# Contrast adjustment on one core: third tile loaded in two pieces, first store held for the larger piece, whole-tile sums on ScalarE for the last three tiles

## The chip, the cores and the metric

The kernel runs on one core of one Trainium2 chip. The metric is the device time of one execution in microseconds (us), as the median of several runs. One execution was also recorded by the hardware profiler; its span runs from the first instruction to the last, and its device time is a little longer than that span.

## The reference

```python
def reference(x, factor):                       # x: (16, 3, 512, 512) float32, factor = 1.5
    mean = np.mean(x, axis=(2, 3), keepdims=True)
    return np.clip(mean + factor * (x - mean), 0, 1).astype(np.float32)
```

There are 48 images (16 batches of 3 channels) of 262,144 pixels each. Every image is stretched around its own mean and cut to 0..1. So every pixel is read once and written once, 50.33 MB each way, and nothing of an image can be written before its mean is known.

## The kernel before

**Tiles.** An image is cut into 16 rows of 16,384 pixels (64 KB each). A tile is 128 such rows, one for each partition, so eight images; there are six tiles of 8.39 MB, numbered 0 to 5. They live in a ring of three buffers (`ring`), so tile 3 takes the buffer of tile 0, and so on: only half of the data is on the chip at a time.

**One tile's work.** `load` (L77) issues the DMA into the ring. `add` sums each row: VectorE reduces the first `SUM` = 4352 columns (L85), and ScalarE copies the other 12,032 columns onto themselves with an accumulated sum (L89). TensorE multiplies the row sums by `blockw`, a 128x128 matrix with (1 - factor)/262144 in blocks of 16x16 (L100), which adds up the 16 rows of each image and gives every partition its image's shift, (1 - factor) * mean, in `bias`. VectorE then makes two passes over the tile in place: times factor plus shift (L103), and the clip to 0..1 (L106). `store` (L80) issues the DMA to `out`.

**Tile 0** is handled in smaller parts so that work starts early. It is loaded in pieces of 8, 24 and 32 KB of each row, summed in two halves, and passed over and stored in two pieces: the first `SHORT` = 2048 columns (8 KB of each row, 1 MB in all), then the other 56 KB of each row.

**Order.** The order is written out by hand (`manual_schedule`): five DMAs load tiles 0 to 2, then the three tiles are computed and stored, then tiles 3 to 5 are loaded, computed and stored. All DMAs, loads and stores alike, are issued by SyncE (SP) on one queue, and SP issues them in program order. A DMA that must wait for an engine or for another transfer (a store for VectorE's clip, a load for the store that frees its buffer) therefore holds up every DMA that stands behind it in SP's order. Each DMA goes over 16 DMA engines, each with eight of the 128 rows, one packet a row.

Of the kernel before, what the change touches and what calls it, by code (L numbers as in the profile page):

```python
# [1 line left out]

# [4 lines left out]


P = 128  # L10
ROW = 16384
HALF = ROW // 2
BUFS = 3
SHORT = 2048
SUM = 4352


@with_exitstack
def kernel(
    ctx: ExitStack,  # L20
    tc: tile.TileContext,
    x: bass.AP,
    factor: float,
    out: bass.AP,
):

    nc = tc.nc
    f32 = mybir.dt.float32  # L30
    Alu = mybir.AluOpType
    Act = mybir.ActivationFunctionType

    B, C, H, W = x.shape
    n_img, n_pix = B * C, H * W
    ppi = n_pix // ROW
    per_tile = P // ppi
    n_tiles = n_img // per_tile
    assert ppi * ROW == n_pix and per_tile * n_tiles == n_img

    factor = float(factor)
    wconst = (1.0 - factor) / float(n_pix)

    x_f = x.rearrange("b c h w -> (b c h w)")
    out_f = out.rearrange("b c h w -> (b c h w)")

    def dram(ap, t, c0=0, c1=ROW):
        return bass.AP(tensor=ap.tensor, offset=t * P * ROW + c0, ap=[[ROW, P], [1, c1 - c0]])

    consts = ctx.enter_context(tc.tile_pool(name="consts", bufs=1))  # L50
    xpool = ctx.enter_context(tc.tile_pool(name="xpool", bufs=1))
    small = ctx.enter_context(tc.tile_pool(name="small", bufs=1))
    psum = ctx.enter_context(tc.tile_pool(name="psum", bufs=1, space=bass.MemoryType.PSUM))


    sums = small.tile([P, 4 * n_tiles], f32, name="sums")
    bias = psum.tile([P, n_tiles], f32, name="bias")

    blockw = consts.tile([P, P], f32, name="blockw")
    blocks = blockw.rearrange("p (a b) -> p a b", b=ppi)  # L60
    nc.gpsimd.memset(blockw, wconst)  # L61
    for base, step in ((0, -ppi), (ppi - 1, ppi)):
        nc.gpsimd.affine_select(  # L63
            out=blocks,
            in_=blocks,
            compare_op=Alu.is_ge,
            fill=0.0,
            base=base,
            pattern=[[step, per_tile], [0, ppi]],
            channel_multiplier=1 if step < 0 else -1,  # L70
        )


    ring = xpool.tile([P, BUFS, ROW], f32, name="ring")

    def load(t, c0=0, c1=ROW):
        nc.sync.dma_start(out=ring[:, t % BUFS, c0:c1], in_=dram(x_f, t, c0, c1))  # L77

    def store(t, c0=0, c1=ROW):
        nc.sync.dma_start(out=dram(out_f, t, c0, c1), in_=ring[:, t % BUFS, c0:c1])  # L80

    def add(t, col, c0, c1, c2):
        xt = ring[:, t % BUFS, :]
        own = sums[:, 4 * t + col : 4 * t + col + 2]
        nc.vector.tensor_reduce(  # L85
            out=own[:, 0:1], in_=xt[:, c0:c1], axis=mybir.AxisListType.X, op=Alu.add
        )
        part = xt[:, c1:c2]
        nc.scalar.activation(out=part, in_=part, func=Act.Copy, accum_out=own[:, 1:2])  # L89
        return [own[:, 1:2], own[:, 0:1]]  # L90

    def compute(t, *cuts):
        xt = ring[:, t % BUFS, :]
        if t == 0:
            parts = add(t, 0, 0, SUM, HALF) + add(t, 2, HALF, HALF + SUM, ROW)
        else:
            parts = add(t, 0, 0, SUM, ROW)
        shift = bias[:, t : t + 1]
        for k, part in enumerate(parts):
            nc.tensor.matmul(shift, blockw, part, start=k == 0, stop=k == len(parts) - 1)  # L100
        for c0, c1 in zip((0, *cuts), (*cuts, ROW)):
            part = xt[:, c0:c1]
            nc.vector.tensor_scalar(  # L103
                out=part, in0=part, scalar1=factor, scalar2=shift, op0=Alu.mult, op1=Alu.add
            )
            nc.vector.tensor_scalar(  # L106
                out=part, in0=part, scalar1=0.0, scalar2=1.0, op0=Alu.max, op1=Alu.min
            )
            store(t, c0, c1)

    with tc.manual_schedule():
        load(0, 0, SHORT)
        load(0, SHORT, HALF)
        load(0, HALF, ROW)
        load(1)
        load(2)
        compute(0, SHORT)
        compute(1)
        compute(2)
        load(3)  # L120
        load(4)
        load(5)
        compute(3)
        compute(4)
        compute(5)


# [1 line left out]
_INS = ['x', 'factor']  # L129
_OUTS = [((16, 3, 512, 512), 'float32')]  # L130

_NUMBERS = {'factor': 1.5}


# [26 lines left out]
```

## Time and profile before

| | |
|---|---|
| median of 3 runs | 239.52 us (239.28 to 239.88) |
| profiled execution | 239.05 us, span 237.3 us |
| bytes | 50.33 MB read, 50.33 MB written |
| VectorE busy | 137.4 us |
| ScalarE busy | 59.9 us |
| TensorE busy | 7.9 us |
| first store issued by SP | at 30.52 us |
| loads of tiles 3, 4, 5 issued | at 94.24, 101.08, 120.82 us |
| stores of tiles 3, 4, 5 issued | at 168.97, 191.81, 214.64 us |

"Busy" counts the time in which an engine executes instructions, and says nothing of whether that time matters. Times of instructions are counted from the start of the span. A DMA has two times of interest: when SP issues it, and when it lands, that is, when its completion is signalled to whoever waits for it. In between it lies in the queue behind earlier DMAs for most of the time: the median load of a whole tile lands 57.7 us after its issue. The view of DMA over time gives, for each slice, the mean busy share of the 16 DMA engines in tenths and what they moved in GB/s; in short slices a packet's bytes are counted where the packet starts.

### The profile page before, as it was taken

What the parts mean: (1) busy time and instruction counts of PE and PEld (TensorE: products, weight loads), DVE (VectorE), ACT (ScalarE), POOL (GpSimd) and SP (SyncE); (2) the same over time, 40 slices, a digit from 0 to 9 for tenths busy, and PEclk for the clock granted to TensorE, in tenths of its full rate; (3) what the DMA queues carried; (4) which work ended last, traced back from release to release, by engine and by line L of the source; (5) the groups of instructions that cost most, each with busy time, mean ns of one, the idle gap of its engine ahead of it and who ended that gap; (6) DMA issues with size and microseconds to landing.
All of it is one profiled execution on the core that took longest, in us unless ns stands there. A gap on an engine that the chain in (4) does not pass through costs nothing.

```text
span 237.3 us, 186 instructions
## 1 busy us (share of the span) xinstructions
PE 7.9 (3%) x28; PEld 6.9 (3%) x28; DVE 137.4 (58%) x21; ACT 59.9 (25%) x15; POOL 1.1 (0%) x7
## 2 busy tenths in 40 slices
PE   0010100010001000000000000100000000000000
PEld 0010100010001000000000000100000000000000
DVE  0071899949998998000000043499989998991000
ACT  2051300980492000000000049319509800000000
POOL 1000000000000000000000000000000000000000
DMA  7999989899799798989899998989899998989894
GB/s 289 418 442 442 530 353 530 353 486 398 331 464 454 341 530 353 530 353 519 365 442 442 398 486 353 530 354 530 353 475 409 431 453 376 508 353 530 353 530 177
DMA packets 2160, 100.66 MB, mean 424 GB/s; under 512 B 240, under 2 KB 240, under 8 KB 240
## 3 DMA queue, kind: packets, MB, share of 16 engines
q1 hardware_dynamic: 2160, 100.66, 98.7%
HBM read 50.33 MB, written 50.33 MB: 424 GB/s over the span
## 4 chain that ended last, share of the span: by engine, by line
DVE 43%; DMA 36%; ACT 9%; PE 2%; SPq 1%; issue 0%; DVEq 0%; ACTq 0%
DMA ring<-in_x_dram 36%; DVE ring L103 18%; DVE ring L106 18%; ACT ring L89 9%; DVE sums L85 6%; PE bias L100 2%; SPq L77 1%; SPq L80 0%; DVEq L103 0%; ACTq L89 0%
## 5 line engine op out<-in xcount | busy, mean ns | idle before, releaser
L89 ACT ACTIVATE ring<-ring 128x12032 f32<-128x12032 f32 (+1 forms) x7 | 58.0, 8280 | 128.2 <-DMA ring<-in_x_dram 128.2
L85 DVE TENSOR_REDUCE sums<-ring 128x1 f32<-128x4352 f32 x7 | 32.8, 4683 | 63.9 <-DMA ring<-in_x_dram 63.9
L103 DVE TENSOR_SCALAR ring<-ring,bias 128x16384 f32<-128x16384 f32 (+2 forms) x7 | 52.8, 7538 | 12.9 <-PE bias L100 12.9
L106 DVE TENSOR_SCALAR ring<-ring 128x16384 f32<-128x16384 f32 (+2 forms) x7 | 52.3, 7476 | 0.2
L100 PE MATMUL bias<-sums,blockw 128*128 128x1 f32 x28 | 7.9, 360 | 189.1 <-ACT ring L89 175.4
L100 PEld LDWEIGHTS bias<-sums,blockw 128*128 128x128 f32 x28 | 6.9, 314 | 190.0 <-ACT ring L89 159.4
L89 ACT ACT_TABLE_LOAD x1 | 1.3, 1283 | 0.8 <-PEq L142 0.8
L89 ACT ACTIVATION_READ_ACCUMULATOR ring<-ring 128x1 f32 x7 | 1.3, 187 | 0.0
L63 POOL TENSOR_SCALAR_AFFINE_SELECT blockw<-blockw 128x128 f32<-128x128 f32 x2 | 0.7, 340 | 0.1
L61 POOL MEMSET blockw<- 128x128 f32 x1 | 0.2, 204 | 0.3 <-POOLq L142 0.3
L142 POOL MEMSET const-bfloat16-1.0<- 128x1 bf16 x1 | 0.1, 102 | 0.0
L142 POOL MEMSET const-uint8-127<- 128x1 uint8 x1 | 0.1, 102 | 0.0
L142 POOL MEMSET const-float32-0.0<- 128x1 f32 x1 | 0.1, 98 | 0.3 <-issue 0.3
L142 POOL MEMSET const-float32-1.0<- 128x1 f32 x1 | 0.1, 98 | 0.0
## 6 DMA issues: line engine op xcount, KB each, us to landing
out_dram<-ring SPq DMA_DIRECT2D x1, 7168.0 KB, 35.9
ring<-in_x_dram SPq DMA_DIRECT2D x1, 4096.0 KB, 20.8
ring<-in_x_dram SPq DMA_DIRECT2D x1, 3072.0 KB, 11.6
ring<-in_x_dram SPq DMA_DIRECT2D x1, 1024.0 KB, 4.7
out_dram<-ring SPq DMA_DIRECT2D x1, 1024.0 KB, 34.3
ring<-in_x_dram SPq DMA_DIRECT2D x5, 57.7
out_dram<-ring SPq DMA_DIRECT2D x5, 27.0
```

The lines of the kernel that those rows point to most:

```text
L61: nc.gpsimd.memset(blockw, wconst)
L63: nc.gpsimd.affine_select(out=blocks, in_=blocks, compare_op=Alu.is_ge, fill=0.0, base=base, pattern=[[step, per_tile], [0, ppi]], channel ...
L77: nc.sync.dma_start(out=ring[:, t % BUFS, c0:c1], in_=dram(x_f, t, c0, c1))
L85: nc.vector.tensor_reduce(out=own[:, 0:1], in_=xt[:, c0:c1], axis=mybir.AxisListType.X, op=Alu.add)
L89: nc.scalar.activation(out=part, in_=part, func=Act.Copy, accum_out=own[:, 1:2])
L100: nc.tensor.matmul(shift, blockw, part, start=k == 0, stop=k == len(parts) - 1)
L103: nc.vector.tensor_scalar(out=part, in0=part, scalar1=factor, scalar2=shift, op0=Alu.mult, op1=Alu.add)
L106: nc.vector.tensor_scalar(out=part, in0=part, scalar1=0.0, scalar2=1.0, op0=Alu.max, op1=Alu.min)
L142: nc = _bacc.Bacc("TRN2", target_bir_lowering=False, num_devices=1)
```

## The change

Three things change.

1. Tile 2 is loaded by two DMAs: the first 58 KB of each row (`ROW - TAIL` = 14,848 columns), then the last 6 KB (`TAIL` = 1536 columns).
2. The first store (the 1 MB piece of tile 0) gets one more thing to wait for: the landing of the 58 KB piece of tile 2. As SP issues in order, the DMAs behind it wait too.
3. For tiles 3 to 5, ScalarE sums all 16,384 columns and VectorE's reduction is left out, so TensorE has one product instead of two. For tiles 0 to 2 the split of the sum stays; only the order in which the two instructions are written, and the columns of `sums` that they use, are exchanged.

```diff
+TAIL = 1536
...
     def add(t, col, c0, c1, c2):
         xt = ring[:, t % BUFS, :]
         own = sums[:, 4 * t + col : 4 * t + col + 2]
+        part = xt[:, c1:c2]
+        nc.scalar.activation(out=part, in_=part, func=Act.Copy, accum_out=own[:, 0:1])
+        if c0 == c1:
+            return [own[:, 0:1]]
         nc.vector.tensor_reduce(
-            out=own[:, 0:1], in_=xt[:, c0:c1], axis=mybir.AxisListType.X, op=Alu.add
+            out=own[:, 1:2], in_=xt[:, c0:c1], axis=mybir.AxisListType.X, op=Alu.add
         )
-        part = xt[:, c1:c2]
-        nc.scalar.activation(out=part, in_=part, func=Act.Copy, accum_out=own[:, 1:2])
-        return [own[:, 1:2], own[:, 0:1]]
+        return [own[:, 0:1], own[:, 1:2]]
 
-    def compute(t, *cuts):
+    def compute(t, *cuts, after=None):
         xt = ring[:, t % BUFS, :]
         if t == 0:
             parts = add(t, 0, 0, SUM, HALF) + add(t, 2, HALF, HALF + SUM, ROW)
         else:
-            parts = add(t, 0, 0, SUM, ROW)
+            parts = add(t, 0, 0, SUM if t < BUFS else 0, ROW)
...
-            store(t, c0, c1)
+            out_dma = store(t, c0, c1)
+            if c0 == 0 and after is not None:
+                tc.add_manual_dep(
+                    out_dma.ins,
+                    after.ins.name,
+                    mybir.DependencyInfo(mybir.DependencyClass.Sync, mybir.DependencyReason.DATA),
+                    reason="the first store follows the loads",
+                )
 
     with tc.manual_schedule():
         load(0, 0, SHORT)
         load(0, SHORT, HALF)
         load(0, HALF, ROW)
         load(1)
-        load(2)
-        compute(0, SHORT)
+        most = load(2, 0, ROW - TAIL)
+        load(2, ROW - TAIL, ROW)
+        compute(0, SHORT, after=most)
```

More of the change, by code (lines that the diff above doesn't have):

```diff
@@ L76, in load @@
     def load(t, c0=0, c1=ROW):
-        nc.sync.dma_start(out=ring[:, t % BUFS, c0:c1], in_=dram(x_f, t, c0, c1))
+        return nc.sync.dma_start(out=ring[:, t % BUFS, c0:c1], in_=dram(x_f, t, c0, c1))
     def store(t, c0=0, c1=ROW):
-        nc.sync.dma_start(out=dram(out_f, t, c0, c1), in_=ring[:, t % BUFS, c0:c1])
+        return nc.sync.dma_start(out=dram(out_f, t, c0, c1), in_=ring[:, t % BUFS, c0:c1])
     def add(t, col, c0, c1, c2):
```

## The prediction

> **What bounds the kernel now.** I read the page first, then the share of each transfer, then the few microseconds around the first change from loading to storing, then the waits around the edits. The page:
>
> ```profile
> span 237.3 us, 186 instructions
> ...
> PE 7.9 (3%) x28; PEld 6.9 (3%) x28; DVE 137.4 (58%) x21; ACT 59.9 (25%) x15; POOL 1.1 (0%) x7
> ...
> q1 hardware_dynamic: 2160, 100.66, 98.7%
> ```
>
> One queue moves 100.66 MB and its packets fill 98.7% of what 16 DMA engines have; VectorE is busy for 58%, ScalarE for 25%. The bound is the queue. The chain of waits credits VectorE with 43%, but that chain follows who issued a DMA; it doesn't show that the queue still had other work. So an edit pays only if it takes time out of the stream of transfers.
>
> That stream runs in order of issue. I cut the span at the landings of its transfers. A landing is an issue plus its time to landing (the page's DMA issues), or the start of the work that waited for it. The windows view (columns: window, its length, busy time of five engines, clock, DMA share, GB/s):
>
> ```profile
> 22.56:41.91 19.35, 1.17 (x4) 1.00 (x4) 18.58 (x5) 3.50 (x2) 0.00 (x0) 1.00 1.00 434
> 41.91:62.38 20.47, 1.01 (x4) 0.93 (x4) 17.36 (x4) 10.32 (x2) 0.00 (x0) 1.00 0.92 375
> ...
> 81.75:101.06 19.31, 0.00 (x0) 0.00 (x0) 11.96 (x2) 0.00 (x0) 0.00 (x0) 1.00 1.00 434
> ...
> 159.12:178.48 19.36, 1.17 (x4) 1.00 (x4) 18.57 (x4) 10.32 (x2) 0.00 (x0) 1.00 1.01 433
> 178.48:197.82 19.34, 1.18 (x4) 1.00 (x4) 18.55 (x4) 10.32 (x2) 0.00 (x0) 1.00 1.00 434
> ```
>
> In order: load of tile 1, load of tile 2, store of tile 1, load of tile 5, store of tile 3. A tile of 8.39 MB takes 19.31 to 19.36 us at 434 GB/s, except tile 2, the last load before the first store: 20.47, which is 1.12 more. (The view books a packet's bytes at its start, so 375 understates that window and the next one overstates.) No other transfer stands out: the two windows left out after the store of tile 1 are 19.74 and 18.96, and sum to two tiles. Outside the stream there is only the start. So 1.12 us is about all that the queue can still give.
>
> Where in tile 2? The DMA view from 50 to 66 us, 40 slices of 0.4 us:
>
> ```profile
> DMA  0390000390000390000590000000279999993003
> GB/s 0 164 2458 0 0 0 0 164 2458 0 0 0 0 164 2458 0 0 0 0 164 2458 0 0 0 0 0 0 0 123 328 430 471 389 410 983 1639 143 0 0 143
> ```
>
> Each pair "164 2458" is the 16 engines starting one 64 KB row. The pairs come six slices apart, 2.4 us. After the last one, at 58.0 to 58.4, the next packets (the 8 KB rows of the first store) only begin at 61.2 and are common from 61.6: the last row of tile 2 held the engines over a microsecond too long. From 61.6 the store runs at some 430 GB/s. That first store was issued at 30.52 and lay behind the loads for 30 us:
>
> ```profile
> 30.52 63.63 SPq L80 DMA_DIRECT2D out_dram<-ring  x4
> ...
> 62.40 10.23 ACT L89 ACTIVATE ring<-ring 128x12032 f32<-128x12032 f32 x1 [10.15 <-DMA ring<-in_x_dram]
> ...
> 168.97 46.01 SPq L80 DMA_DIRECT2D out_dram<-ring  x3
> ```
>
> The other change from loading to storing, at 178.5, also had its store queued early (168.97), with rows of 64 KB, and lost nothing (19.36, then 19.34). So what disturbs seems to be many small store rows that wait right behind the last load row.
>
> **The change part by part.**
>
> *First store held until 58 KB of each row of tile 2 have landed.* At the stream's rate, 58 of 64 KB take 19.35 x 58/64 = 17.54 us, so that part lands at 41.91 + 17.54 = 59.45. SP goes on 0.02 us after a landing (the load of tile 5 was issued at 120.82; the store before it landed at 93.82 + 27.0 = 120.82, at 120.80 by the cut). The first store is then issued at 59.47 instead of 30.52, after nearly all of tile 2 is in. What this removes: up to 1.12 us.
>
> Its price is the risk that the queue runs dry. 6 KB of each row are left as cover: 19.35 x 6/64 = 1.81 us. The only row with an issue into an empty queue is the first load: issued at 0.80, 1 MB, landed 4.7 us later. If the first store needed as long, it would land at 59.47 + 4.7 = 64.17. In an unbroken stream tile 2 is in at 41.91 + 19.35 = 61.26 and the store's 1 MB (8.39 MB in 19.35 gives 2.42) lands at 63.68. The gap would be 0.49. The other end is 0: the engines are running, not cold, and the store reads on-chip memory. Below 0 is excluded, since 434 GB/s is the most that any cut shows. I take the middle, 0.25, because the one row is like in size and row length but is a load at a cold start.
>
> Can the disturbance remain in part? The first load's packets began at 1.8 us (DMA view of the first 8 us), 1.0 after issue, so the store's rows could reach an engine from 60.5 on, and tile 2's data end by about 60.9: tile 1 landed at 41.91, but its last rows had given way to tile 2's by 41.5 (the pair at 50.4 to 51.2, less four rows of 2.42), so a landing comes some 0.4 us after the data, and 61.26 - 0.4 = 60.9. The overlap is at most some 0.4 of a row's 2.42 us, or 0.4/2.42 x 1.12 = 0.19 us. It comes on an engine in place of the gap, not on top, so 0 to 0.49 stays the span of both.
>
> Queued behind the waiting store on SP are the second store (ready at 45.8), the store of tile 1 (ready at 70.9), and the later loads from 94.2. The second store then issues at about 59.9, and the stream needs it at 63.7 less the 1 us of lead; it is covered by 2.8 us. Nobody else moves. VectorE and ScalarE never wait for a store in this half, and the loads that reuse the buffers are issued at 94.24 as before, set by VectorE's end at 93.75.
>
> *Load of tile 2 in two pieces.* One more issue on SP, 0.4 us at 2.8 to 3.3 us, hidden behind 60 us of loads. The second piece has 6 KB rows. The nearest row is the store of tile 0, split in 1 MB and 7 MB: landings at 30.52 + 34.3 = 64.82 and 45.82 + 35.9 = 81.72, from 62.40, so 19.32 in all, as an unsplit store. Cost 0, at most a few hundredths.
>
> The Trainium skill speaks against this piece: "DMA: Bandwidth & Descriptors", section "Rules for kernel authors", asks for at least 1 MiB per DMA, and "Anatomy of one DMA" (the GpSimd path) charges a fixed 2.0 us or so for each (fitted on DMAs issued from GpSimd). The piece has 0.75 MiB; at that price the sum would be about 240.65. The two store pieces above show no such fee inside a full queue, and the trace decides.
>
> *ScalarE adds tiles 3 to 5 whole.* ScalarE takes 10.23 us for 12032 columns and 3.40 for 3840, so (10.23 - 3.40)/8192 = 0.834 ns a column and 13.86 us for 16384. VectorE loses three reductions of 4.68, TensorE three pairs of instructions. Per tile: landing, 13.86, 0.19 for the accumulator, 0.05, one product 0.60, 0.11, then VectorE's 17.49 and 0.07 to the store's issue. Tile 3 (landing 139.76 - 0.87 = 138.89): store issued at 171.3, before 168.97; the stream reaches it when load 5 lands, at 177.6. Tile 4 (158.25): 190.6, before 191.8; due at 197.0. Tile 5 (177.6): 210.0, before 214.64; due at 216.3. Every store stays queued 6 us ahead, so all of it lies under the transfers: cost 0 and gain 0. If that cover were gone, tile 3 would cost 2.3 us (3.2 counted from the earlier landing). The other order of the two adds within a tile changes no engine's own order.
>
> **Sum.** 1.12 - 0.25 = 0.87. The profiled execution had 239.05 us, a span of 237.30 and 1.75 around it; after the change its span would be 236.43 and its time 238.18. The median of the runs is 0.47 above it, so 239.52 - 0.87 = **238.65 us**. With 0.49 of gap it is 238.89, with none 238.40.
>
> **The rivals.**
>
> *The 1.12 us is the first store's own start, not its place behind the loads* (slower). It is the first write to `out`, and the second change of direction, which shows none, is not the first. Then the cost stays, and the wait adds its gap: 239.52 + 0.49 = 240.0. The wait loses from the point where gap and what is left of the cost exceed 1.12. Passing 0.3% (0.72 us here, about what a measurement of this kernel can tell from no change) needs a lead of the store 0.23 us longer than the first load's. Against it: the late bytes are those of the load, and the store's packets run at full rate from the first slice.
>
> *The disturbance moves to the 6 KB rows.* The store's 8 KB rows reach engines that still have small load rows in hand and cost half or more of the 1.12: 239.0 to 239.5. For it: store rows are as small as before, and an engine can be up to 0.4 us behind another. Against it: the overlap is short.
>
> *The change does nothing.* Holding the store doesn't matter, since the late row has another cause, such as VectorE's pass over tile 1 from 53.4 to 71 (columns as many were processed from 76 to 94 with the queue at 434, which speaks against it): 239.5.
>
> **How the numbers follow.** The forecast gets 0.60, the first-store rival 0.20, the moved disturbance 0.15, nothing 0.05. Faster than 238.80 are 0.57 from the forecast and 0.01 from the edge of the moved disturbance, 0.58. Slower than 240.24 is half of the first-store rival, 0.10. The rest, 0.32, is within 0.3%. The forecast's own range is 238.4 to 238.9; to leave out no more than 2 in 10 it has to take in the second and third rival and the near edge of the first: 238.3 to 239.8.
>
> **What the next profile would show.** Right: the first store issued near 59.5, ScalarE on tile 2 near 61.3 instead of 62.40, tile 2's 58 KB rows evenly spaced at 2.2 us with no empty microsecond after the last, store of tile 0's first piece landed by 64.0, all later landings 0.9 earlier, and stores of tiles 3 to 5 issued near 171.3, 190.6 and 210.0 with the DMA share still about 1. It is wrong if the slices between 60.5 and 62 hold more than 0.5 us without packets (lead too long), if tile 2's last piece lands after 61.8 (disturbance still there), or if any store after 170 us is issued after the queue has reached it.

## The result, and the profile after

The changed kernel is slower: a median of 240.19 us (239.52 to 241.94, 14 runs) beside 239.40 (239.07 to 239.88, 14 runs) of the kernel before, a ratio of 1.0041 with a 95% interval of 1.0028 to 1.0054. The forecast was 238.65 us in a range of 238.3 to 239.8. A second set of runs gave 241.02 (6 runs), 1.0065 (1.0052 to 1.0078). The runs also scatter more than those of the kernel before: three of the 14 took 241.30 to 241.94 us, the other eleven 239.52 to 240.42.

The profiled execution took 241.83 us, with a span of 240.1; that is one of the three, so its profile shows the losses at their larger end. A second profile below is milder (240.84 us), but none of the eleven was profiled. The page first, with the lines that answer to those of before:

```profile
span 240.1 us, 167 instructions
...
PE 6.3 (3%) x22; PEld 5.4 (2%) x22; DVE 123.6 (51%) x18; ACT 70.8 (29%) x15; POOL 1.1 (0%) x7
...
q1 hardware_dynamic: 2304, 100.66, 97.9%
```

VectorE is 13.8 us less busy and ScalarE 10.9 more, as the third edit says, and none of it reached the span. The queue moves the same bytes, and its packets fill 97.9% of the span where they filled 98.7%. In windows cut at the landings (the order is load of tile 1, load of tile 2, store of tile 1, store of tile 2, load of tile 3, load of tile 5, store of tile 3):

```profile
22.70:42.05 19.35, 1.17 (x4) 1.00 (x4) 18.58 (x5) 3.50 (x2) 0.00 (x0) 1.00 0.99 428
42.05:61.46 19.41, 1.02 (x4) 0.93 (x4) 16.33 (x3) 10.32 (x2) 0.00 (x0) 1.00 0.94 402
80.88:100.21 19.33, 0.00 (x0) 0.00 (x0) 12.96 (x2) 0.00 (x0) 0.00 (x0) 1.00 1.00 434
100.21:120.42 20.21, 0.00 (x0) 0.00 (x0) 0.00 (x0) 0.00 (x0) 0.00 (x0) 1.00 0.99 412
120.42:140.80 20.38, 0.00 (x0) 0.00 (x0) 0.00 (x0) 0.00 (x0) 0.00 (x0) 1.00 0.96 415
160.12:181.33 21.21, 0.59 (x2) 0.50 (x2) 19.36 (x3) 13.95 (x2) 0.00 (x0) 1.00 1.06 439
181.33:200.68 19.35, 0.59 (x2) 0.50 (x2) 15.64 (x3) 13.95 (x2) 0.00 (x0) 1.00 1.01 437
```

The second line is the success: tile 2 takes 19.41 us where it took 20.47. The others are where it went: the store of tile 2 takes 20.21 (before 19.74), the load of tile 3 20.38 (18.96), the load of tile 5 21.21 (19.36). The two windows of the kernel before for the store of tile 2 and the load of tile 3:

```profile
101.06:120.80 19.74, 0.00 (x0) 0.00 (x0) 0.00 (x0) 0.00 (x0) 0.00 (x0) 1.00 0.98 425
120.80:139.76 18.96, 0.00 (x0) 0.00 (x0) 0.00 (x0) 0.00 (x0) 0.00 (x0) 1.00 1.02 442
```

All three longer windows lie at the two later changes of direction, from storing to loading at about 120 us and from loading to storing at about 178. VectorE and ScalarE did nothing at all from 100 to 140.

The DMA view from 50 to 66 us (40 slices of 0.4) shows the first crossing as it was meant to be:

```profile
DMA  9300399000993003990002899899999999000093
GB/s 1485 148 0 0 148 1485 742 0 0 0 891 1336 148 0 0 148 1782 445 0 0 0 108 353 492 430 369 425 425 471 410 389 410 1720 881 0 0 0 0 2150 143
```

The starts of the 58 KB rows come in bursts 2.2 us apart, then at 58.4 the 6 KB rows begin at about 430 GB/s, and the 8 KB rows of the first store follow at 60.5 with no empty slice. The store was issued at 59.70, and its wait on SP reads in the waits view as:

```profile
SPq L81 <- DMA ring<-in_x_dram: 55.7, 1, 55.7
```

Now the second crossing, the same view from 112 to 128 us, before and then after:

```profile
DMA  9900009900009930009930009930009970009970
GB/s 983 1638 0 0 0 0 983 1638 0 0 0 0 983 1475 164 0 0 0 983 1475 164 0 0 0 983 1475 164 0 0 0 655 1638 328 0 0 0 655 1638 328 0
```

```profile
DMA  0000790000990000009900403900303930303930
GB/s 0 0 0 0 328 2294 0 0 0 0 328 2294 0 0 0 0 0 0 1147 1311 0 0 164 0 164 2294 0 0 164 0 164 2130 164 0 164 0 164 2130 164 0
```

Before, every burst of row starts follows the last by six slices (2.4 us), straight through the crossing. After, the burst at 116.0 is followed by the next at 119.2, eight slices later: the last row of the store of tile 2 held its engine for most of a microsecond too long. One engine fell behind the others as well (the lone 164 three slices, 1.2 us, behind each burst, first at 120.8).

To compare kernels I take a **loss at a crossing**: the time between two landings around it, less what the transfers between take in an undisturbed stretch (19.345 us for the load of a tile, 19.30 for the store of one at the second crossing and 19.31 at the third, 2.43 for 1 MB). A landing here is when a DMA's completion is counted; each of the 16 engines counts by itself, and the table gives the median engine and, after the stroke, the last one, which sets the end. A crossing is a change of direction, and "held" means held as in the change, behind a piece of 58 KB of each row with 6 KB left as cover, unless the table says otherwise. All in us, from one profile each.

| kernel | first crossing (61) | second (120) | third (178) | ratio to before, 95% interval |
|---|---|---|---|---|
| before | 1.07 / 1.16 | 0.03 / 0.06 | 0.06 / 0.04 | |
| the change | 0.15 / 0.12 | 0.87 / 1.97 | 0.90 / 1.84 | 1.0041 (1.0028 to 1.0054) |
| the change, second profile | 0.27 / 0.29 | 0.97 / 1.46 | 0.95 / 1.33 | 1.0065 (1.0052 to 1.0078) |
| split and hold alone | 0.52 / 0.34 | 0.82 / 1.73 | 0.97 / 1.34 | 1.0068 (1.0052 to 1.0084) |
| ScalarE edit alone | 1.49 / 1.56 | 0.02 / -0.02 | 0.17 / 0.10 | 0.9998 (0.9989 to 1.0006) |
| split alone | 1.35 / 1.32 | 0.05 / 0.10 | 0.03 / 0.19 | 0.9993 (0.9984 to 1.0002) |
| hold with 24 KB of cover | 1.56 / 1.56 | 0.03 / 0.05 | 0.22 / 0.46 | 1.0002 (0.9993 to 1.0011) |
| first and third held | 0.27 / 0.31 | 1.02 / 1.59 | 0.58 / 0.10 | 1.0032 (1.0022 to 1.0043) |
| second alone held | 1.40 / 1.43 | 0.70 / 0.99 | 1.13 / 1.52 | 1.0089 (1.0075 to 1.0103) |
| all three held | 0.56 / 0.77 | 1.02 / 1.04 | 0.33 / 0.23 | 1.0009 (0.9998 to 1.0019) |
| stores held in mid-stream, 6 KB of cover | 1.41 / 1.42 | 0.84 / 0.99 | 0.97 / 1.21 | 1.0101 (1.0078 to 1.0123) |
| the same, 24 KB of cover | 1.35 / 1.34 | 0.01 / 0.02 | 0.03 / 0.05 | 0.9997 (0.9988 to 1.0006) |
| small store at 42 us | 1.64 / 1.71 | 0.05 / 0.06 | 0.04 / 0.06 | 1.0001 (0.9992 to 1.0009) |
| small store at 5 us | 0.34 / 0.54 | -0.02 / 0.09 | 0.07 / 0.22 | 1.0021 (1.0008 to 1.0035) |

The profile's span grew by 2.8 us, and the last engine's terms add up to it: -1.04 at the first crossing, +1.91 at the second, +1.80 at the third, and 0.14 of a later start, 2.81 in all.

### The profile page after: what moved, and what is told of

It is laid out like the page before. It is cut to its first block, busy times and chain, and to the rows that moved or that the text cites. A ratio compares the mean times of both kernels' runs of the same rounds, so it can differ in the third digit from the quotient of the medians.

```text
span 240.1 us, 167 instructions
## 1 busy us (share of the span) xinstructions
PE 6.3 (3%) x22; PEld 5.4 (2%) x22; DVE 123.6 (51%) x18; ACT 70.8 (29%) x15; POOL 1.1 (0%) x7
## 3 DMA queue, kind: packets, MB, share of 16 engines
q1 hardware_dynamic: 2304, 100.66, 97.9%
## 4 chain that ended last, share of the span: by engine, by line
issue 29%; ACT 17%; DVE 7%; another core or an unknown queue 5%; PE 0%; ACTq 0%
ACT ring L87 17%; DVE ring L106 4%; DVE ring L109 4%; PE bias L103 0%; ACTq L87 0%; ACTq L167 0%
## 5 line engine op out<-in xcount | busy, mean ns | idle before, releaser
L87 ACT ACTIVATE ring<-ring 128x16384 f32<-128x16384 f32 (+2 forms) x7 | 68.8, 9834 | 123.8 <-issue 69.1
L90 DVE TENSOR_REDUCE sums<-ring 128x1 f32<-128x4352 f32 x4 | 18.7, 4682 | 18.0 <-DMA ring<-in_x_dram 18.0
L103 PE MATMUL bias<-sums,blockw 128*128 128x1 f32 x22 | 6.3, 360 | 189.7 <-ACT ring L87 185.3
L103 PEld LDWEIGHTS bias<-sums,blockw 128*128 128x128 f32 x22 | 5.4, 314 | 190.5 <-ACT ring L87 169.2
```

The source lines that it names most:

```text
L90: nc.vector.tensor_reduce(out=own[:, 1:2], in_=xt[:, c0:c1], axis=mybir.AxisListType.X, op=Alu.add)
```

## The experiments

All of them are edits of the kernel before, except where the change itself is the base.

**Which edit does it?** Three parts of the change, and the change again. The hold without the ScalarE edit:

```diff
-            parts = add(t, 0, 0, SUM if t < BUFS else 0, ROW)
+            parts = add(t, 0, 0, SUM, ROW)
```

> The split load and the held first store, without the ScalarE edit (tiles 3 to 5 are summed by VectorE and ScalarE as before). Theory A (the toll moves): a change of direction of the queue costs about 1 us when the 16 DMA engines cross it in step with the next transfer already queued; the first crossing of the kernel before pays it and spreads the engines, which lets the two later crossings off; the hold keeps the engines in step, so both later ones pay. Then this run is as slow as the full change: 0.2 to 0.6% over before, tile 2 in at about 61.3 and the store of tile 2, or load of tile 3 behind it, and the load of tile 5 each late by 0.5 to 1.2 us. Theory B (the ScalarE edit causes the later losses): 0.3 to 0.45% faster than before (about 238.5), later transfers 19.3 to 19.4 each. Theory C (the losses are drawn at random in each execution): neither pattern, and the losses differ from those of the full change in place and size.

Measured: 241.12 us, 1.0068, a little over the expectation's 0.6%. The pattern is that of the full change, which took 241.02 us in the same set of runs. The edit on ScalarE has no part in it.

The ScalarE edit without split and hold:

```diff
-        most = load(2, 0, ROW - TAIL)
-        load(2, ROW - TAIL, ROW)
-        compute(0, SHORT, after=most)
+        load(2)
+        compute(0, SHORT)
```

> The ScalarE edit alone: tile 2 in one load, first store not held. Theory A: no difference from before (within 0.15%), the first crossing pays about 1.1 us (tile 2 takes 20.4 to 20.5) and the later ones under 0.4 each. Theory B: slower than before by 0.4 to 1%, with the load of tile 5 or store of tile 3 late. Theory C: within 0.4% of before on either side, losses at other places.

Measured: 239.36 us, 0.9998. The first crossing cost 1.49, more than the expectation's 1.1. The store of tile 3 was issued at 172.28 instead of 168.97, still 6 us before the stream reached it. Its first crossing, in the DMA view from 50 to 66, has the same hole as before:

```profile
GB/s 0 1638 983 0 0 0 0 1638 983 0 0 0 0 1475 1147 0 0 0 0 1475 1147 0 0 0 0 0 0 0 0 205 389 512 369 410 492 1372 1167 0 0 0
```

The split without the hold (on top of the first edit above):

```diff
-        compute(0, SHORT, after=most)
+        compute(0, SHORT)
```

> Tile 2 loaded in 58 and 6 KB of each row, but the first store is not held, and no ScalarE edit. Theory A: the first store is queued early, so the first crossing pays as before (0.8 to 1.2 us) and the later ones little; time within 0.2% of before. If the toll needs a 64 KB row just ahead of the crossing, the first crossing is cheap here and the later ones pay, and the time is that of the full change, 0.2 to 0.6% over before.

Measured: 239.28 us, 0.9993. With the store queued early, the first crossing costs 1.35 although the rows just ahead of it have 6 KB. It is the hold that matters, not the pieces.

The change again:

> The changed kernel again, for a second profile and more times. Theory A: the same three places as in its first profile: first crossing cheap (tile 2 complete at about 61.3), 0.5 to 1.2 us lost at the end of the store of tile 2 and again at the end of the load of tile 5; time 0.3 to 0.5% over before. Theory C: the losses sit elsewhere, or differ by more than half a microsecond in size.

Measured: 241.02 us, 0.65% over before where 0.3 to 0.5% was expected, with the losses in the same places and of the same size on the median engine. The last engine was 0.51 us less late than in the first profile at both later crossings. So the places are not drawn by chance (Theory C); what the last engine loses does vary from run to run.

Theory A as it stood there fell with these profiles too, in one point. It said that a crossing is dear when the engines reach it in step. In the ScalarE edit alone all engines lost 1.4 to 1.6 us alike at the first crossing, so their spread stayed at 0.5 to 0.6 us, and the later crossings were free; in the hold alone the landings at the second crossing were about as far apart (0.4 us), and it was dear. So I replaced "in step" by a lead: that each engine reads ahead of its writes (theory A2 in what follows).

**Hold other crossings.** The pieces of a store and the hold of a later DMA were made like those of the change:

```diff
-        load(5)
-        compute(3)
+        most5 = load(5, 0, ROW - TAIL)
+        load(5, ROW - TAIL, ROW)
+        compute(3, after=most5)          # third crossing held
...
-        compute(2)
-        load(3)
+        put = compute(2, pieces=True)    # store of tile 2 in 58 and 6 KB
+        hold(load(3), put)               # second crossing held
```

First and third:

> Sums as before. The first crossing from loads to stores is held as in the change (58 and 6 KB of tile 2), and the third crossing in the same way (tile 5 loaded as 58 and 6 KB, the store of tile 3 held for the 58 KB part). Theory A2 (lead): each DMA engine reads ahead of its writes; a crossing from loads to stores with the stores queued costs about 1 us once and leaves a lead that lets the later crossings off; a held crossing costs 0.1 to 0.2 but leaves no lead, so the next crossing from stores to loads pays about 1 us. Then here the first is cheap, the second pays about 1 us as in the hold alone, the third is cheap: 1 us less than the hold alone, 239.5 to 240.1. Theory D (the hold disturbs the rest of the run in some other way): as slow as the hold alone, about 241, the third late by 0.8 or more in spite of its hold.

Measured: 240.20 us, 1.0032, a little over the range. The third crossing no longer hurts the last engine (0.10 instead of 1.34), though the median engine still loses 0.58; the second costs as before. Against the hold alone it is 0.36% better, 0.86 us.

The second alone:

> Sums and first crossing as before (not held). Only the second crossing, from the store of tile 2 to the load of tile 3, is held: the store of tile 2 goes in 58 and 6 KB pieces and the load of tile 3 waits for the 58 KB piece to land. Theory A2: the first crossing pays 1.0 to 1.5, the second has a gap of 0.2 to 0.8, and the lead is lost, so that the third, free in the kernel before, now pays 0.8 to 1.2: 240.2 to 241. Rival E (the cost is paid once in an execution, by whichever crossing comes first with its transfers queued): the third stays under 0.4, 239.5 to 240.1.

Measured: 241.81 us, 1.0089, above the range of A2 and far from that of E. The kernel before had a free third crossing; here, with nothing changed at it, it costs 1.13 / 1.52. In the DMA view from 170 to 186 the bursts are six slices apart up to 176.0 and then the next comes after nine:

```profile
GB/s 0 0 0 1802 655 164 0 0 0 1638 655 328 0 0 0 1475 819 328 0 0 0 0 0 0 1475 819 164 164 0 0 1475 819 164 164 0 0 1475 819 164 164
```

So the cost isn't paid once for all; what the first crossing bought was lost again at the hold.

All three:

> Sums as before; all three crossings held by 58 and 6 KB pieces. Theory A2: 0.1 to 0.2 at the first and third; at the second a gap of 0.2 to 0.8, since a load out of an empty read-ahead has the longer way: 238.6 to 239.3, the fastest so far. Theory D: 240 or more, with losses of 0.8 or more in spite of the holds.

Measured: 239.67 us, 1.0009: the best of the kernels held with 6 KB of cover, but a miss for the expectation. The held second crossing costs 1.02, not 0.2 to 0.8, so here going from stores to loads pays about one microsecond whether it is held (1.02) or not (0.82 in the hold alone), once the queue has been let run short ahead of it.

**Wait long before the crossing.** The hold of the change, without the ScalarE edit, with another cover:

```diff
-TAIL = 1536
+TAIL = 6144
```

> As the hold alone, but the cover is 24 KB of each row instead of 6 (TAIL = 6144): the first store is held until 40 KB of each row of tile 2 have landed, and then waits in the queue for some 7 us of loads. Theory A2: what matters is that the store is in the queue well ahead of the crossing, not how long: the first crossing pays 0.9 to 1.5, the later two under 0.4 each, time within 0.2% of before. Theory D (the wait itself, or the order of issue that it makes, disturbs the rest): first cheap or not, the later two late by 0.5 to 1.2 each as in the hold alone, 240 to 241.

Measured: 239.43 us, 1.0002. The store still waits for a landing on SP, for 23 us longer than before (issued at 53.88), and nothing is lost or won: the first crossing pays its usual price (1.56, a little over the expectation). A hold costs only where the queue has little left behind it.

**Run short away from any crossing.** If a queue that nearly runs dry loses the lead, it should do so in the middle of the stores as well:

```diff
-        compute(1)
-        compute(2)
+        put = compute(1, pieces=True)    # store of tile 1 in two pieces
+        compute(2, after=put)            # store of tile 2 waits for the first of them
```

> Sums, loads and the first crossing as before (not held). The store of tile 1 goes in 58 and 6 KB pieces and the store of tile 2 is held until the 58 KB piece has landed: the queue runs short of work at about 100 us, in the middle of the stores, at no crossing. Theory A2 (a queue that runs short loses the read-ahead, wherever that is): the first crossing pays 1.0 to 1.5 as before, the handover at 100 costs under 0.3, and then the crossing to loads at 120 pays about 1 us and the one to stores at 178 too: 240.4 to 241.6. Rival F (what is lost is lost only where a crossing itself is held): the later crossings cost under 0.4 each, 239.3 to 239.9.

Measured: 241.70 us, 1.0101, 0.1 us above the range of A2. Its control:

```diff
-TAIL = 1536
+TAIL = 6144
```

> The control for the run short of work in the middle of the stores: the same wait with 24 KB of each row as cover (40 and 24 KB pieces), so that the store of tile 2 is queued some 6 us before it is needed. Theory A2: the queue never runs short and the time is that of before within 0.15%, one loss of 1.0 to 1.5 at the first crossing. If the split or the wait by itself does the harm: 0.3 to 0.8% slower.

Measured: 239.34 us, 0.9997. The two profiles side by side, DMA view from 112 to 128 us, first with 6 KB of cover and then with 24 KB:

```profile
DMA  0990000990000990000099930009970009970009
GB/s 0 1311 1311 0 0 0 0 1147 1475 0 0 0 0 655 1966 0 0 0 0 0 492 983 983 164 0 0 0 655 1638 328 0 0 0 492 1802 328 0 0 0 492
```

```profile
DMA  0990000990000990000990000990000990000990
GB/s 0 2130 492 0 0 0 0 2130 492 0 0 0 0 1638 983 0 0 0 0 1147 1475 0 0 0 0 1147 1475 0 0 0 0 983 1638 0 0 0 0 819 1802 0
```

With 24 KB the bursts keep their six slices through the crossing at 120. With 6 KB the burst at 117.2 is followed by one smeared from 120.0 to 121.6. The handover at 100 us itself cost 0.0 to 0.1 on any engine. And at the third crossing, from 170 to 186, again 6 KB and then 24 KB:

```profile
GB/s 0 0 0 1311 1147 164 0 0 0 1311 1147 164 0 0 0 1147 1147 328 0 0 0 0 0 328 1475 492 328 0 0 328 1475 492 328 0 0 328 1475 492 328 0
```

```profile
GB/s 0 1966 655 0 0 0 0 1966 655 0 0 0 0 1966 655 0 0 0 0 1475 1147 0 0 0 0 1475 1147 0 0 0 0 1311 1311 0 0 0 0 1147 1475 0
```

Rival F is out: the harm needs no held crossing, only a queue that runs short. In this pair the last piece of the store shrinks together with the cover. For a load, the split alone showed that a 6 KB piece without a hold does no harm; for a store no run has one without a hold.

**Pay early with a small store.** One extra store of 64 KB of constants, on the base of the kernel before, into a place that the last store writes again:

```diff
+    def small_store():
+        nc.sync.dma_start(out=dram(out_f, n_tiles - 1, 0, P), in_=blockw)
...
         load(1)
+        small_store()       # or behind load(0, 0, SHORT)
```

Behind the load of tile 1:

> The kernel before with one extra store of 64 KB in all (128 rows of 512 bytes of the constant weights, into a part of the output that its own store writes again at the end), queued between the load of tile 1 and the load of tile 2. This puts a crossing from loads to stores with the store queued ahead at about 41.9 us. Theory A2 (a queued crossing from loads to stores costs about 1 us once and leaves a state that lets the later crossings off): the cost moves to 41 to 43 us, the load of tile 2 behind it takes 19.3 to 19.7, and the first real crossing at 61 to 63 costs under 0.3; time within 0.25% of before. If a store as small as this leaves no such state: about 1 us lost at both places, 240.2 to 240.8. If only the first real store pays (cold output): nothing at 42, 1.1 at 61, 239.4 to 239.7.

Measured: 239.59 us, 1.0001, and none of the three expectations. The small store cost 0.19 us from landing to landing and the first real crossing lost some 1.45 (the table's 1.64 has both). So a crossing of two directions as such costs nothing there, a store that small leaves nothing either, and it is not the first write to the output that is dear.

Behind the first piece of tile 0:

> The same extra store of 64 KB, queued right behind the first load piece (the issue of the second piece waits for the constants, so it comes about 1 us later than before). Theory A2: the cost of the first crossing is paid at 5 to 7 us, while the engines are still starting, and all three real crossings cost under 0.3 each; if the start hides a part of it, the run is faster than before by up to 0.4% (238.5 to 239.4). If the state needs a larger store: the crossing at 61 costs 1.0 to 1.5 as before, 239.5 to 240.8.

Measured: 239.81 us, 1.0021. Here something seems to have been paid early: the second piece of tile 0 landed 8.1 us after the transfer ahead of it instead of 7.3, and the first real crossing then lost 0.34 instead of 1.07. 0.8 and 0.34 make 1.1: the sum stayed, and only its place moved. The 0.8 is not a gap: the second piece was issued 1.01 us later than before (at 2.25 us), but on the median engine its rows began at 5.05 us where they began at 4.98, and then took 0.7 us more. Whether the later issue had a part in that no run shows. Neither expectation fits: the run is not faster, and the crossing at 61 did not cost 1.0 to 1.5. Why the same small store buys most of it at 5 us and nothing at 42 is open.

## Why the prediction was wrong

**The first crossing: right in size, and only in part in mechanism.** The wait bound (SP's 55.7 us on the load), tile 2 came 1.06 us sooner in the windows, and the queue did not run visibly dry. The first crossing went from 1.07 to 0.15 on the median engine, a gain of 0.92 where the sum had 0.87. The 0.25 us for the gap lies inside the 0.15 to 0.56 that the five profiles with this hold show. But the reason, many small store rows behind the last load row, fails: the third crossing of the change has rows of 64 KB on both sides and lost 0.90. One more reading is off: 434 GB/s, by which a gap below 0 was excluded, is not the most that any cut shows (the windows view has 442 and 470, with bytes counted at a packet's start). No profile went below 0 at the first crossing all the same.

**The ScalarE edit: right.** Stores of tiles 3 to 5 were issued at 173.09, 192.40 and 213.56, as worked out and shifted by the lost time, each still well ahead of the stream. Alone it moved nothing (0.9998).

**The split: right.** Alone 0.9993. The Trainium skill, "DMA: Bandwidth & Descriptors", section "Rules for kernel authors", asks for at least 1 MiB per DMA; a piece of 0.75 MiB cost nothing here while the queue behind it was full.

**The step that failed** is the sentence "Nobody else moves", and the reading under it. I took the two later crossings, free in the trace of before, as a property of theirs, and the 1.12 us as a disturbance local to the first. The third crossing was even read as proof that only small store rows disturb. In fact whether they are free depends on what the queue went through before them. The sum had one term for the hold (0 to 0.49 of gap) where two more were due: 0.8 to 1.0 us each on the median engine, at 120 and at 178, and on the last engine up to 1.97. They outweigh the 0.92 us won at the first.

**What the runs show in its place.** The cost of a crossing depends on what the queue went through before. (1) The first crossing from loads to stores costs 1.1 to 1.6 if the stores are queued ahead, and then the later ones cost 0.0 to 0.2 on the median engine: before, ScalarE edit, split, both 24 KB covers, small store at 42 us. (2) If the queue is let run short, the crossings behind that point cost about 1 us each again: both later ones in the change and in the mid-stream run, the second itself and the third in the second-alone run, and in these last two runs the first had been paid in full. A third crossing that was itself held cost 0.3 to 0.6 there. (3) With 24 KB of cover the same waits do nothing.

A picture that fits this: an engine's reads run ahead of its writes. A queued crossing from loads to stores would stall the writes once, while the reads go on, and that lead would hide the longer way of the reads at later crossings. A queue that runs short would let the writes catch up, and reads and writes then go at one rate, so the lead doesn't come back by itself. "DMA: Bandwidth & Descriptors", section "Two DMAs through the same engine are not ordered", says that the read and the write side of an engine are separate queues.

The packet records of the traces hold one more sign. On the median engine the store of tile 2 landed 0.7 to 0.8 us after the record of its last row had ended in all seven profiles whose second crossing was free, and 0.3 to 0.4 us after it in all seven whose second crossing cost 0.70 or more. Other whole tiles land 0.3 to 0.4 us after their last row. In the kernel before, the rows of that store ended at 119.74, those of the load of tile 3 began at 119.75, and the store landed at 120.53; this is why the two windows there are 19.74 and 18.96, which the prediction passed over because they sum to two tiles. In the change the last row of the store took 3.15 us instead of 2.42, and its landing followed 0.35 us later. So where the crossing is free, the completion of the store is late and the loads go on; where it is dear, the row itself is long. That is what a lead would look like, but the records don't say which side of an engine they time, and the third crossing shows no such difference. The lead stays argued; that the state exists, where it is lost and what it is worth is shown.

**The rivals.** The slower rival came out on the right side with the wrong mechanism: it had the cost stay at the first store, where it fell to 0.15. Nor is the 1.12 us the first write to the output (the small store at 42 us wrote first, and the first real crossing still lost some 1.45). The moved disturbance had the right word and the wrong place: it moved 60 and 120 us on, not onto the 6 KB rows. Its chance of 0.15 would have been better spent on a rival that asks who profits from the loss.

**Better than both?** None was found. Holding all three crossings removes about what it adds (1.0009), and the early small store did not make the run faster (1.0021). Where the queue stays full, one loss of 1.1 to 1.6 us is about the whole price of the three crossings. No profile here paid less in all than that of the kernel before, 1.16 us on the median engine, if the 0.8 at the start of the early small store is counted.

## What to carry to other kernels

A queue that never runs short may be worth more than the hole that you see in it: before a loss is cut out, ask what the same event does for the places that are free of loss, and make a rival of "this was paid once for all of them". Hold a DMA back only with a cover several times its lead (24 KB of each row, 7 us, did no harm; 6 KB, 1.8 us, did, although no empty slice was to be seen; nothing between was measured). After such an edit, cut the whole span at the landings again, not only the place that was edited.

## What the runs showed of the hardware that was not expected

- A crossing of direction in a full queue costs 0.0 to 0.2 us or about 1 us, by the history of the queue and not by its own transfers alone: the third, with the same transfers, cost 0.06 in the kernel before and 1.13 behind a held second.
- The history can be spoiled without a visible loss: at 100 us in the mid-stream run the handover took 0.1 us at most, and the bill of 0.84 and 0.97 (median engine) came 20 and 78 us later.
- A spoiled queue also lets single engines fall behind: the last of the 16 lost 1.97 at the second crossing of the change where the median lost 0.87. With a DMA spread over all engines, the last one sets the time.
